# Hybrid decoder layer on one core: start-up loads split over two queues, casts ordered by hand, squares behind them

## The chip, the cores and the metric

The kernel runs on one core of a Trainium2 chip. PE is TensorE (matrix products), DVE is VectorE, ACT is ScalarE, POOL is GpSimd, SP is SyncE, which here only issues DMAs. The metric is the device time in microseconds (us) of one execution, as the median of several runs.

## The reference

One layer of a hybrid decoder for 1024 prompt tokens and 64 sample tokens (8 sequences of 8), all in float32, model width 1024. One normalised input feeds a retention mixer (8 heads, with recurrent state and gate) and a sliding-window attention (8 query heads, 2 key/value heads, window 128, ALiBi, sinks, normalised q and k). Then come an output projection, a residual, and a squared-ReLU MLP of width 4096 with its own norm and residual.

```python
hn = rms_norm(x, norm_mix_gain)
proj = hn @ w_in
q_r, k_r, v_r, g_r, q_s, k_s, v_s = jnp.split(proj, cuts, axis=-1)
o_r, new_ret = retention(q_r, k_r, v_r, ret_state, chunk)
o_r = rms_norm(o_r).reshape(b, t, RET_WIDTH) * jax.nn.silu(g_r)
q_s = rms_norm(q_s.reshape(b, t, N_SWA_HEADS, HEAD_DIM), q_norm_gain)
k_s = rms_norm(k_s.reshape(b, t, N_SWA_KV, HEAD_DIM), k_norm_gain)
...
h = x + jnp.concatenate([o_r, o_s], axis=-1) @ w_out
hf = rms_norm(h, norm_ffn_gain)
h = h + jnp.square(jax.nn.relu(hf @ w_up)) @ w_down
```

## The kernel before

**Products.** A float32 product is made of three passes in a reduced format: each operand is split into a high part (`hi`, a cast on ACT) and the rest (`lo`, a subtraction on DVE, or on POOL for some weights). `mm3` (L171 to L174) then issues hi x hi, lo x hi and hi x lo into one PSUM bank; so L172, L173 and L174 are the lines of nearly all PE work, and the name of the bank tells which product it is.

**Tiles of the front.** The 1088 tokens lie in three chunks of 384, 384 and 320 columns (`CH`), the 1024 channels in eight pieces of 128 partitions. `load_x` (L90) loads some pieces of one chunk, `wload` (L63) the weights of one block of 256 output columns: raw rows into a ring of three buffers, hi on ACT (L77), lo (L79). The first block is wq0, the first half of the attention's query weights; its 128x2048 come in four quarters q0 to q3. `split_scaled` (L134) multiplies an x piece by the norm gain `g_mix` and splits it: `hnh` on ACT (L136), `hnl` on DVE (L137). The row's rms factor is not needed for these products; it is applied later, and its input is gathered beside them: `square_sum` (L139) squares a piece on ACT (the first piece straight into `rsb`, L143; the others into `sqm`, L146) and DVE adds `sqm` to `rsb` (L147). The buffer of `sqm` is one of three (tag `ntmp`, pool `nt`), which the squares of the q products (`sqq`) share.

**Products of the front.** `proj_q` (L262) multiplies wq0 with all three chunks into banks `psq`; for each it makes on ACT a square `sqq` (L268), on DVE a scaled copy `qs` (L271), and on PE column sums `prq` (L152) of `sqq`, which DVE copies to `rq` (L286). Then the key and value weights `wkv` are loaded and split, and `proj_tok` multiplies them with the token tiles into `pst` (L307). The banks of the pool `psA` (three) are shared: the first `pst` uses the bank of the first `psq` and needs it to be emptied.

**Order of issue.** SP's queue carries all loads of the front in this order: g_mix (`cload`, L58), x piece 0, q0, x piece 1, q1, x pieces 2-3, q2, x pieces 4-5, q3, x pieces 6-7, then chunk 1 in two loads of four pieces, chunk 2 in two, and constants. ACT issues nothing there; its first instruction is the load of an activation table, with a small activation (`warm`, L86) behind it. The program's order of splits and squares is the loop at L202: the splits of a chunk, then the squares of the chunk before.

**Who sets the final order.** The kernel is built with a scheduler (`TC_KW`) that orders each engine's instructions on its own, by dependences and its estimates of durations, for the whole program. `tc.issue_after(ins)` holds an instruction behind another one. So an edit in the front can change the order in later stages whose code is the same.

**A later stage of that kind.** Between 300 and 500 us retention runs block by block, with the value products (bank `pst`, weights `wv`) between. A block loads q, k and gate (`qt`, `kt`, `gt`, L543 to L546), splits q and k (L701 to L706), makes scores `rsr`, the transposed keys `pkr` (L599), the outputs `ror`, the state update `pur` (L737), and its normalised output is transposed to `pm` (L767), gated and split (`mixrh` on ACT, `mixrl` on POOL, L779). Then the output projection begins: raw rows of W_out are loaded (`wor_raw` for the retention half, `woa_raw` for the attention half, L819), split (`wor`, `woa`, L787 and L788) and multiplied with the mixers' outputs (`mixr`, and `mixa`, which L811 loads from DRAM) into banks `pso`.

Of the kernel before, what the change touches and what calls it, by code (L numbers as in the profile page):

```python
# [11 lines left out]
F32 = mybir.dt.float32  # L12
F32R = mybir.dt.float32r
AF = mybir.ActivationFunctionType
ALU = mybir.AluOpType
# [5 lines left out]
P = 128  # L21
# [4 lines left out]
CH = ((0, 384), (384, 384), (768, 320))  # L26
# [10 lines left out]
def hymba_layer(ctx: ExitStack, tc: tile.TileContext, a: dict, o: dict):  # L37
    nc = tc.nc
# [6 lines left out]
    ring = proj.enter_context(tc.tile_pool(name="ring", bufs=2, side="right", reuse_waits="tile"))  # L45
# [5 lines left out]
    def slot3(i, dt, name, cw):  # L51
        return slot(i, dt, name)[:, : 8 * cw].rearrange("p (k n) -> p k n", k=8)
# [2 lines left out]
        t_ = hnp.tile([P, 8 * cw], F32R, tag=f"hn{x}{c}", name=f"hn{x}{c}")  # L55
        return t_.rearrange("p (k n) -> p k n", k=8)

    def cload(name):  # L58
        t_ = const.tile(list(a[name].shape), F32, name="c_" + name)
        nc.sync.dma_start(t_, a[name])  # L60
        return t_

    def wload(src, kk, name, lo_eng="p", parts=2, after=()):  # L63
        hi = ring.tile([P, 2048], F32R, tag="whi", name=name + "_hi")
        lo = ring.tile([P, 2048], F32R, tag="wlo", name=name + "_lo")
        n = 2048 // parts
        after = list(after)
        for h in range(2):
            raw = ring.tile([P, 1024], F32, tag="raw", name=f"{name}_raw{h}", bufs=3)
            for q in range(0, 1024, n):  # L70
                nc.sync.dma_start(raw[:, q : q + n], src[:, h * 1024 + q : h * 1024 + q + n])
                if after:
                    load_x(*after.pop(0))
            for q in range(0, 1024, n):
                h_, l_ = (v[:, h * 1024 + q : h * 1024 + q + n] for v in (hi, lo))
                r_ = raw[:, q : q + n]
                nc.scalar.copy(h_, r_)  # L77
                eng = nc.vector if lo_eng[(2 * h + q // n) % len(lo_eng)] == "v" else nc.gpsimd
                eng.tensor_tensor(l_, r_, h_.bitcast(F32), ALU.subtract)  # L79
        return hi.rearrange("p (k n) -> p k n", k=kk), lo.rearrange("p (k n) -> p k n", k=kk)  # L80


    ones = const.tile([P, 64], F32, name="ones")
    nc.vector.memset(ones, 1.0)
    warm = const.tile([P, 1], F32, name="warm")
    nc.scalar.activation(warm, ones[:, 0:1], AF.Silu)  # L86
    g_mix = cload("g_mix")
    xs = [slot3(6 + c, F32, f"x{c}", cw) for c, (c0, cw) in enumerate(CH)]

    def load_x(c, k, n):  # L90
        c0, cw = CH[c]
        nc.sync.dma_start(
            xs[c][:, k : k + n, :],
            a["xT"][:, 8 * c0 + k * cw : 8 * c0 + (k + n) * cw].rearrange("p (k n) -> p k n", k=n),
        )

    load_x(0, 0, 1)
    w_q0 = wload(a["w_in"][0], 8, "wq0", "v", 4, ((0, 1, 1), (0, 2, 2), (0, 4, 2)))
    load_x(0, 6, 2)
    for c in (1, 2):  # L100
        for k in (0, 4):
            load_x(c, k, 4)

    g_ffn = cload("g_ffn")
    qkg = cload("qkg")
    sinks = cload("sinks")
    ident = cload("ident")
# [25 lines left out]

    def split_scaled(src, gain, hi, lo):  # L134

        nc.scalar.activation(hi, src, AF.Copy, scale=gain)  # L136
        nc.vector.scalar_tensor_tensor(lo, src, gain, hi.bitcast(F32), ALU.mult, ALU.subtract)  # L137

    def square_sum(acc, src, k, nm):  # L139

        cw = src.shape[-1]
        if k == 0:
            nc.scalar.activation(acc, src, AF.Square)  # L143
        else:
            sq = nt.tile([P, 512], F32, tag="ntmp", name=f"sq{nm}_{k}")
            nc.scalar.activation(sq[:, :cw], src, AF.Square)  # L146
            nc.vector.tensor_tensor(acc, acc, sq[:, :cw], ALU.add)  # L147
# [23 lines left out]
    def mm3(ps, lh, ll, rh, rl, first, last, more=False):  # L171
        nc.tensor.matmul(ps, lh, rh, start=first, stop=False, skip_group_check=more)  # L172
        nc.tensor.matmul(ps, ll, rh, start=False, stop=False, skip_group_check=more)  # L173
        return nc.tensor.matmul(ps, lh, rl, start=False, stop=last, skip_group_check=more)  # L174
# [22 lines left out]
    def squares_of(c):  # L197
        c0, cw = CH[c]
        for k in range(8):
            square_sum(rsb[:, c0 : c0 + cw], xs[c][:, k, :], k, f"m{c}")  # L200

    for c, (c0, cw) in enumerate(CH):  # L202
        hi, lo = hn[c]
        for k in range(8):
            split_scaled(xs[c][:, k, :], g_mix[:, k : k + 1], hi[:, k, :], lo[:, k, :])
        if c:
            squares_of(c - 1)
    def proj_tok(t, w, ps):

        _, c, r = tok_tile(t)  # L210
        hi, lo = hn[c]
        for k in range(8):
            lh, ll = hi[:, k, r : r + 128], lo[:, k, r : r + 128]
            mm3(ps[:, :256], lh, ll, w[0][:, k, :], w[1][:, k, :], k == 0, k == 7)
        return ps
# [85 lines left out]


    w = wload(a["w_in"][2], 8, "wkv", "v")
    for t in range(9):
        off, c, r0 = tok_tile(t)
        rt = rst[:, t : t + 1]
        ps = proj_tok(t, w, psA.tile([P, 512], F32, tag="mm", name="pst"))  # L307
        sq = sp.tile([P, 128], F32, tag="hsq", name="hsq")
        nc.scalar.activation(sq, ps[:, :128], AF.Square, scale=rt)
# [24 lines left out]
        if t == 8:  # L334
            nc.vector.tensor_scalar(k8[:, 128:192], pt[:, 64:128], qkg[:, 1:2], None, ALU.mult)
            nc.vector.tensor_scalar(v8, ps[64:128, 128:256], rt[64:128], None, ALU.mult)

    proj_q(1, wload(a["w_in"][1], 8, "wq1", "v"))
    nc.sync.dma_start(o["kp"], k8[:, 0:128])
    nc.sync.dma_start(o["vp"], vs[:, 7, :])  # L340
# [102 lines left out]
    s_, r_ = rq8[:, 0:4], rq8[:, 4:8]  # L443
# [62 lines left out]
    for blk in range(4):  # L506
        w = wload(a["w_in"][3 + blk], 8, f"wqk{blk}")
# [9 lines left out]
    for blk in range(2):  # L517
        w = wload(a["w_in"][7 + blk], 8, f"wg{blk}")
# [67 lines left out]
    def value_block(t):  # L586
        vt = vts[t] = rv.tile([P, 512], F32, tag="vt", name=f"vtr{t}", bufs=5)
        _, c, r = tok_tile(t)
        ps = psA.tile([P, 512], F32, tag="mm", name="pst")
        for k in range(8):  # L590
            lh, ll = (x[:, k, r : r + 128] for x in hn[c])
            ins = mm3(ps, lh, ll, w_v[k // 4][0][:, k % 4, :], w_v[k // 4][1][:, k % 4, :], k == 0, k == 7)
        nc.scalar.activation(vt, ps, AF.Copy, scale=rst[:, t : t + 1])
        return ins.ins
# [348 lines left out]
    for t in range(5):  # L943
        if t == 0:
            for _ in range(2):
                ins = queued(ins, next, decode)
            ins = queued(ins, value_block, 3)
            for _ in range(2):
                ins = queued(ins, next, decode)
# [3 lines left out]
        if t:  # L953
            ins = queued(ins, value_block, t + 3)
# [253 lines left out]
    for g, (f0, nf) in enumerate(((0, 2), (2, 4), (6, 4), (10, 4), (14, 2))):  # L1208
# [7 lines left out]
        for i in DOWN:  # L1216
# [17 lines left out]
            for m in range(4):  # L1234
                for s in range(2):
# [143 lines left out]
```

## Time and profile before

| what | value |
|---|---|
| median of 3 runs | 1193.63 us (1193.47 to 1195.85) |
| profiled execution | 1199.06 us |
| its span in the trace | 1197.3 us |
| mean granted PE clock | 0.993 |
| instructions | 23489 |
| PE busy over the span | 98% |
| DMA over the span | 142 GB/s |

The span runs from the first to the last event of the trace; the other 1.76 us of the profiled execution lie around it. Times in the profile count from the span's start. In a row of waits or of the timeline, `<-` behind a bracket or a name tells whose end the engine waited for. SPq is SP's queue of DMA issues, PEld the loading of weights into PE.

### The profile page before, as it was taken

Reading aid. Unit: us, or ns where it says so; the run is one execution under the profiler, and the core shown is the slowest. Engines: PE = TensorE matmul, PEld = TensorE weight load, DVE = VectorE, ACT = ScalarE, POOL = GpSimd, SP = SyncE. Lnnn points to the kernel's source line nnn. Section 1 sums busy time; section 2 is a strip of 40 time slices with the busy share of each in tenths; the row PEclk is TensorE's granted clock in tenths of the full one; section 3 lists DMA queues with packets and bytes.
Section 4 is the critical chain, followed back from the end, with each engine's and each line's share of the span. In section 5 each row is a group of like instructions: output and inputs, shape, how many; then the busy total and the mean of one; then the engine's idle time right before and its main releaser. Section 6 shows DMA issues by size and latency. Waiting matters only on the chain.

```text
span 1197.3 us, 23489 instructions
## 1 busy us (share of the span) xinstructions
PE 1178.0 (98%) x9405; PEld 1129.8 (94%) x9405; DVE 842.7 (70%) x1546; ACT 513.2 (43%) x1055; POOL 491.2 (41%) x393
## 2 busy tenths in 40 slices
PE   8999999999999999998999999999999999999998
PEld 7999988988778999998999999999999999999998
DVE  7556868632356969887766766667688779897676
ACT  8343545543233437644444444444552332424231
POOL 0125333333334632456666766667372133053000
PEclk9999999999899999999999999999999999999999
DMA  7211235243226654344443444434775456553215
GB/s 245 71 62 68 92 102 174 94 134 105 76 71 222 204 166 157 120 136 137 147 150 122 147 142 147 156 127 156 245 258 164 136 170 193 172 167 104 76 58 187
DMA packets 102276, 169.44 MB, mean 142 GB/s; under 512 B 11999, under 2 KB 68255, under 8 KB 101911
## 3 DMA queue, kind: packets, MB, share of 16 engines
q1 hardware_dynamic: 88279, 123.24, 30.7%
q10 hardware_dynamic: 11328, 35.79, 9.3%
q0 software_dynamic: 2560, 8.91, 2.4%
q8 instruction: 74, 1.21, 0.4%
q14 instruction: 35, 0.29, 0.1%
HBM read 114.30 MB, written 53.61 MB: 140 GB/s over the span
## 4 chain that ended last, share of the span: by engine, by line
PE 80%; DVE 8%; DMA 4%; issue 4%; POOL 2%; ACT 2%; ACTq 0%; SPq 0%; DVEq 0%; POOLq 0%
PE psd L173 8%; PE psd L174 8%; PE psd L172 8%; PE psx L173 5%; PE psx L172 5%; PE psx L174 4%; PE pst L172 2%; PE psz L173 2%; PE psz L172 2%; PE pst L173 2%; PE psz L174 2%; PE pst L174 2%; PE psf L172 2%; PE psf L174 2%; PE pso L174 2%
## 5 line engine op out<-in xcount | busy, mean ns | idle before, releaser
L174 PE MATMUL psd<-ul,wd_w 128*128 128x272 f32 x896 | 258.6, 289 | 2.0 <-DVE ul L788 2.0
L173 PE MATMUL psd<-uh,wd_w 128*128 128x272 f32 x896 | 259.9, 290 | 0.4 <-DVE wd_w L788 0.4
L172 PE MATMUL psd<-uh,wd_w 128*128 128x272 f32 x896 | 258.6, 289 | 0.6 <-ACT uh L787 0.6
L174 PEld LDWEIGHTS psd<-ul,wd_w 128*128 128x128 f32 x896 | 169.2, 189 | 2.9 <-DVE ul L788 2.9
L172 PEld LDWEIGHTS psd<-uh,wd_w 128*128 128x128 f32 x896 | 169.8, 189 | 0.8 <-ACT uh L787 0.8
L173 PEld LDWEIGHTS psd<-uh,wd_w 128*128 128x128 f32 x896 | 169.1, 189 | 0.8 <-DVE wd_w L788 0.7
L1248 DVE TENSOR_TENSOR a<-a,psd 128x272 f32<-128x272 f32 x248 | 101.4, 430 | 41.9 <-PE psd L174 41.8
L788 DVE TENSOR_TENSOR wu_w<-wu_s,wu_w 128x512 fp32r<-128x512 f32 x64 | 61.8, 967 | 52.5 <-ACT wu_w L787 51.7
L787 ACT CAST wd_w<-wd_s 128x512 fp32r<-128x512 f32 x64 | 37.3, 618 | 111.4 <-PE psd L174 99.3
L788 DVE TENSOR_TENSOR ul<-ur,uh 128x1088 fp32r<-128x1088 f32 x56 | 83.5, 1520 | 1.7 <-ACT uh L787 1.7
L172 PE MATMUL psx<-op_1h,wu_w 128*128 128x272 f32 x256 | 74.3, 290 | 3.0 <-ACT m L1125 3.0
L1111 DVE SCALAR_TENSOR_TENSOR m<-m,rsf 128x272 f32<-128x272 f32 x96 | 74.1, 771 | 3.1 <-ACT rsf L910 0.5
L173 PE MATMUL psx<-op_1h,wu_w 128*128 128x272 f32 x256 | 74.7, 292 | 0.0
L173 PE MATMUL psx<-op_0h,wu_w 128*128 128x272 f32 x256 | 74.5, 291 | 0.0
L174 PE MATMUL psx<-op_1l,wu_w 128*128 128x272 f32 x256 | 74.3, 290 | 0.0
L172 PE MATMUL psx<-op_0h,wu_w 128*128 128x272 f32 x256 | 74.0, 290 | 0.3 <-ACT m L1125 0.3
L174 PE MATMUL psx<-op_0l,wu_w 128*128 128x272 f32 x256 | 74.0, 289 | 0.0
L787 ACT CAST uh<-ur 128x1088 fp32r<-128x1088 f32 x56 | 59.7, 1101 | 15.4 <-PE psd L173 9.1
L362 POOL TENSOR_TENSOR sp<-sp,ssp 128x1024 f32<-128x1024 f32 (+1 forms) x16 | 28.6, 1787 | 88.4 <-DVE ssp L361 60.0
L172 PE MATMUL psf<-hnh,wqk_hi 128*128 128x384 f32 (+1 forms) x192 | 63.5, 331 | 0.2 <-DVE qkst L514 0.2
L174 PE MATMUL psf<-hnl,wqk_hi 128*128 128x384 f32 (+1 forms) x192 | 63.1, 329 | 0.0
L173 PE MATMUL psf<-hnh,wqk_lo 128*128 128x384 f32 (+1 forms) x192 | 62.8, 327 | 0.0
(342 smaller groups left out, 3629.2 us busy)
## 6 DMA issues: line engine op xcount, KB each, us to landing
ur<-u_d SPq DMA_DIRECT2D x52, 544.0 KB, 5.0
u_d<-r4t SPq DMA_DIRECT2D x32, 544.0 KB, 4.3
wu_r<-in_w_up ACTq DMA_DIRECT2D x32, 512.0 KB, 4.4
wd_r<-in_w_down ACTq DMA_DIRECT2D x30, 512.0 KB, 6.6
u_d<-r3t SPq DMA_DIRECT2D x32, 408.0 KB, 2.7
y<-in_xY POOLq DMA_DIRECT2D x16, 272.0 KB, 3.5
y_d<-y POOLq DMA_DIRECT2D x16, 272.0 KB, 2.9
yt<-y_d SPq DMA_DIRECT2D x16, 272.0 KB, 3.5
```

What stands on the lines that cost most here:

```text
L172: nc.tensor.matmul(ps, lh, rh, start=first, stop=False, skip_group_check=more)
L173: nc.tensor.matmul(ps, ll, rh, start=False, stop=False, skip_group_check=more)
L174: return nc.tensor.matmul(ps, lh, rl, start=False, stop=last, skip_group_check=more)
L362: nc.gpsimd.tensor_tensor(s, s, ss.unsqueeze(2).broadcast_to([P, 4, n]), ALU.mult)
L787: nc.scalar.copy(hi, src)
L788: lo_eng.tensor_tensor(lo, src, hi.bitcast(F32), ALU.subtract)
L1111: nc.vector.scalar_tensor_tensor(t_, src, 0.0, rsf[:, s, h, :], ALU.max, ALU.mult)
L1248: nc.vector.tensor_tensor(to, to, ps, ALU.add)
```

## The change

It does five things in the code of the front:

1. `g_mix` and the quarters q0 and q1 are loaded from ACT's queue, ahead of its table load; the other loads stay on SP, in the order x piece 0, x piece 1, q2, x pieces 2-3, q3, x pieces 4-5, x pieces 6-7.
2. Chunk 1 is loaded in three parts: pieces 0-1, 2-3, 4-7.
3. The hi casts of the first chunk and of wq0 are chained on ACT by `issue_after` in the order x0, q0, x1, q1, x2, x3, q2, x4, x5, q3, x6, x7.
4. The squares of a chunk may be issued only behind the last of these casts.
5. `wload` loses the argument that put x loads between its own.

```diff
-    def cload(name):
+    def cload(name, eng=nc.sync):
         t_ = const.tile(list(a[name].shape), F32, name="c_" + name)
-        nc.sync.dma_start(t_, a[name])
+        eng.dma_start(t_, a[name])
...
+    g_mix = cload("g_mix", nc.scalar)
+    raw_q0 = [ring.tile([P, 1024], F32, tag="raw", name=f"wq0_raw{h}", bufs=3) for h in range(2)]
+
+    def load_q0(q, eng):
+        eng.dma_start(raw_q0[q // 2][:, q % 2 * 512 : q % 2 * 512 + 512], a["w_in"][0][:, q * 512 : q * 512 + 512])
+
+    for q in (0, 1):
+        load_q0(q, nc.scalar)
     ones = const.tile([P, 64], F32, name="ones")
     nc.vector.memset(ones, 1.0)
     warm = const.tile([P, 1], F32, name="warm")
     nc.scalar.activation(warm, ones[:, 0:1], AF.Silu)
-    g_mix = cload("g_mix")
...
     load_x(0, 0, 1)
-    w_q0 = wload(a["w_in"][0], 8, "wq0", "v", 4, ((0, 1, 1), (0, 2, 2), (0, 4, 2)))
+    load_x(0, 1, 1)
+    load_q0(2, nc.sync)
+    load_x(0, 2, 2)
+    load_q0(3, nc.sync)
+    load_x(0, 4, 2)
     load_x(0, 6, 2)
-    for c in (1, 2):
-        for k in (0, 4):
-            load_x(c, k, 4)
+    for c, k, n in ((1, 0, 2), (1, 2, 2), (1, 4, 4), (2, 0, 4), (2, 4, 4)):
+        load_x(c, k, n)
...
-    for c, (c0, cw) in enumerate(CH):
+    def split_x(c, k):
         hi, lo = hn[c]
+        return split_scaled(xs[c][:, k, :], g_mix[:, k : k + 1], hi[:, k, :], lo[:, k, :])
...
+    def split_q0(q):
+        h_, l_ = (v[:, q * 512 : q * 512 + 512] for v in (wq_hi, wq_lo))
+        r_ = raw_q0[q // 2][:, q % 2 * 512 : q % 2 * 512 + 512]
+        ins = nc.scalar.copy(h_, r_)
+        nc.vector.tensor_tensor(l_, r_, h_.bitcast(F32), ALU.subtract)
+        return ins.ins
+
+    ins = split_x(0, 0)
+    for f_, args in (
+        (split_q0, (0,)), (split_x, (0, 1)), (split_q0, (1,)), (split_x, (0, 2)), (split_x, (0, 3)), (split_q0, (2,)),
+        (split_x, (0, 4)), (split_x, (0, 5)), (split_q0, (3,)), (split_x, (0, 6)), (split_x, (0, 7)),
+    ):
+        with tc.issue_after(ins):
+            ins = f_(*args)
+    w_q0 = [v.rearrange("p (k n) -> p k n", k=8) for v in (wq_hi, wq_lo)]
+    for c in (1, 2):
         for k in range(8):
-            split_scaled(xs[c][:, k, :], g_mix[:, k : k + 1], hi[:, k, :], lo[:, k, :])
-        if c:
+            split_x(c, k)
+        with tc.issue_after(ins):
             squares_of(c - 1)
```

What the scheduler makes of it shows in the order of the instructions. In the following rows a number behind a name is a buffer's, and lines of the changed kernel lie some 30 below those of the kernel before.

DVE at the end of the front, before: the adds of chunk 1's squares (`sqm_3` to `sqm_7`), the last x splits, the two halves of `wkv_lo`, and the first copies `qs`.

```order
L147 TENSOR_TENSOR rsb<-rsb,sqm_3_249 128x384
L137 SCALAR_TENSOR_TENSOR hnl_165<-x_77,c_g_mix,hnh_164 128x320 x4
L147 TENSOR_TENSOR rsb<-rsb,sqm_4_252 128x384
L137 SCALAR_TENSOR_TENSOR hnl_165<-x_77,c_g_mix,hnh_164 128x320 x4
L147 TENSOR_TENSOR rsb<-rsb,sqm_5_255 128x384
L79 TENSOR_TENSOR wkv_lo<-wkv_raw_612,wkv_hi 128x1024
L147 TENSOR_TENSOR rsb<-rsb,sqm_6_258 128x384
L79 TENSOR_TENSOR wkv_lo<-wkv_raw_616,wkv_hi 128x1024
L235 MEMSET q2v 128x512
L147 TENSOR_TENSOR rsb<-rsb,sqm_7_261 128x384
L271 TENSOR_SCALAR qs_267<-psq,qg_115 128x384 x2
```

The same place after:

```order
L155 TENSOR_TENSOR rsb<-rsb,sqm_1_244 128x384
L144 SCALAR_TENSOR_TENSOR hnl_156<-x_81,c_g_mix,hnh_155 128x320 x4
L155 TENSOR_TENSOR rsb<-rsb,sqm_2_247 128x384
L76 TENSOR_TENSOR wkv_lo<-wkv_raw_613,wkv_hi 128x1024
L76 TENSOR_TENSOR wkv_lo<-wkv_raw_617,wkv_hi 128x1024
L155 TENSOR_TENSOR rsb<-rsb,sqm_3_250 128x384
L155 TENSOR_TENSOR rsb<-rsb,sqm_4_253 128x384
L155 TENSOR_TENSOR rsb<-rsb,sqm_5_256 128x384
L264 MEMSET q2v 128x512
L155 TENSOR_TENSOR rsb<-rsb,sqm_6_259 128x384
L300 TENSOR_SCALAR qs_268<-psq,qg_106 128x384
L155 TENSOR_TENSOR rsb<-rsb,sqm_7_262 128x384
```

The adds no longer stand one by one between splits but three in a row behind `wkv_lo`, and the last one stands behind the first `qs`. Further up, the adds 1, 2, 3 and 4, 5 of chunk 0 also stand in a row now, behind all splits of that chunk; before, only 2 and 3 did, and the add of `sqm_1` stood between the splits of pieces 1 and 2. On ACT the squares 3 to 7 of chunk 1 stand in a row between the second cast of `wkv_hi` and the first `sqq`; before, they alternated with x splits and the two casts.

SP where W_out's first rows are loaded, before:

```order
L544 DMA kt_4088<-kr_d 128x4x128
L546 DMA gt_4091<-g_d 128x4x128
L543 DMA qt_4243<-qr_d 128x4x128
L819 DMA wor_0_raw<-in_w_out 128x2x512
L819 DMA woa_0_raw<-in_w_out 128x2x512
L811 DMA mixah_4226<-ms_hi_d 128x4x544
L811 DMA mixal_4228<-ms_lo_d 128x4x544
L544 DMA kt_4244<-kr_d 128x4x128
L819 DMA woa_2_raw<-in_w_out 128x2x512
L546 DMA gt_4247<-g_d 128x4x128
```

and after:

```order
L572 DMA qt_4244<-qr_d 128x4x128
L573 DMA kt_4245<-kr_d 128x4x128
L575 DMA gt_4248<-g_d 128x4x128
L848 DMA wor_0_raw<-in_w_out 128x2x512
L848 DMA woa_0_raw<-in_w_out 128x2x512
L840 DMA mixah_4227<-ms_hi_d 128x4x544
L840 DMA mixal_4229<-ms_lo_d 128x4x544
L572 DMA qt_4462<-qr_d 128x4x128
```

The key and gate loads of the next block (`kt_4245`, `gt_4248`) went ahead of W_out's first rows and of the attention output. A key load waits until PE has transposed the block whose buffer it takes, a gate load until POOL has done `mixrl` of an earlier block.

PE at the first product with W_out, before:

```order
L174 MATMUL pst<-wv_lo,hnh_164 128x512
L767 MATMUL pm<-c_ident,mtr_3924 128x128 x4
L599 MATMUL pkr_3997<-c_ident,kt_3968 128x128 x4
L722 MATMUL ror_4004<-vtr_3606,rptr_3986 64x64 x8
L722 MATMUL ror_4004<-vtr_3606,rptr_3995 64x64 x8
L730 MATMUL ror_4004<-state_3386,qdr_4021 128x128 x4
L737 MATMUL pur_4027<-vtr_3606,kdr_4002 64x64 x8
L172 MATMUL pso<-mixrh,wor_0_4218 128x272
```

and after, from the transposes `pkr` on:

```order
L628 MATMUL pkr_3998<-c_ident,kt_3969 128x128 x4
L751 MATMUL ror_4005<-vtr_3607,rptr_3987 64x64 x8
L751 MATMUL ror_4005<-vtr_3607,rptr_3996 64x64 x8
L759 MATMUL ror_4005<-state_3387,qdr_4022 128x128 x4
L182 MATMUL pst<-wv_lo,hnh_155 128x512
L180 MATMUL pst<-wv_hi,hnh_155 128x512
L181 MATMUL pst<-wv_hi,hnl_156 128x512
L182 MATMUL pst<-wv_lo,hnh_155 128x512
L766 MATMUL pur_4028<-vtr_3607,kdr_4003 64x64 x8
L180 MATMUL rsr_4256<-qkb 128x256
L180 MATMUL rsr_4265<-qkb 128x256
```

Four value products and the scores `rsr` of the next block (ten more of its products follow) now lie between the transposes and the first `pso`.

More of the change, by code (lines that the diff above doesn't have):

```diff
@@ L56, in hn_tile, with wload @@
         return t_.rearrange("p (k n) -> p k n", k=8)
-    def cload(name):
+    def cload(name, eng=nc.sync):
         t_ = const.tile(list(a[name].shape), F32, name="c_" + name)
-        nc.sync.dma_start(t_, a[name])
+        eng.dma_start(t_, a[name])
         return t_
-    def wload(src, kk, name, lo_eng="p", parts=2, after=()):
+    def wload(src, kk, name, lo_eng="p", parts=2):
         hi = ring.tile([P, 2048], F32R, tag="whi", name=name + "_hi")
@@ L66, in wload @@
         n = 2048 // parts
-        after = list(after)
         for h in range(2):
@@ L71, in wload @@
                 nc.sync.dma_start(raw[:, q : q + n], src[:, h * 1024 + q : h * 1024 + q + n])
-                if after:
-                    load_x(*after.pop(0))
             for q in range(0, 1024, n):
@@ L134, in split_scaled @@
     def split_scaled(src, gain, hi, lo):
-        nc.scalar.activation(hi, src, AF.Copy, scale=gain)
+        ins = nc.scalar.activation(hi, src, AF.Copy, scale=gain)
         nc.vector.scalar_tensor_tensor(lo, src, gain, hi.bitcast(F32), ALU.mult, ALU.subtract)
+        return ins.ins
     def square_sum(acc, src, k, nm):
@@ L200, in squares_of @@
             square_sum(rsb[:, c0 : c0 + cw], xs[c][:, k, :], k, f"m{c}")
-    for c, (c0, cw) in enumerate(CH):
+    def split_x(c, k):
         hi, lo = hn[c]
+        return split_scaled(xs[c][:, k, :], g_mix[:, k : k + 1], hi[:, k, :], lo[:, k, :])
+    wq_hi, wq_lo = (ring.tile([P, 2048], F32R, tag="w" + x, name="wq0_" + x) for x in ("hi", "lo"))
+    def split_q0(q):
[3 more added lines that the diff above has]
+        nc.vector.tensor_tensor(l_, r_, h_.bitcast(F32), ALU.subtract)
+        return ins.ins
+    ins = split_x(0, 0)
[7 more added lines that the diff above has]
+    for c in (1, 2):
         for k in range(8):
-            split_scaled(xs[c][:, k, :], g_mix[:, k : k + 1], hi[:, k, :], lo[:, k, :])
-        if c:
+            split_x(c, k)
+        with tc.issue_after(ins):
             squares_of(c - 1)
```

## The prediction

> **What bounds the kernel now.** I read the page's engine line first, then the busy time by stretches of the span, because a share over 1197 us says nothing about the first 40, where the change works.
>
> ```profile
> PE 1178.0 (98%) x9405; PEld 1129.8 (94%) x9405; DVE 842.7 (70%) x1546; ACT 513.2 (43%) x1055; POOL 491.2 (41%) x393
> ```
>
> The columns of the stretches are: length, then busy time (and instructions) of PE, PEld, DVE, ACT and POOL, then the granted clock, the DMA share and GB/s.
>
> ```profile
> 0.00:5.00 5.00, 3.67 (x36) 3.53 (x36) 0.56 (x3) 2.52 (x4) 0.82 (x15) 1.00 0.48 123
> 5.00:10.00 5.00, 2.87 (x13) 2.06 (x14) 2.79 (x6) 3.06 (x6) 0.00 (x0) 1.00 0.94 313
> 10.00:20.00 10.00, 9.75 (x50) 8.27 (x50) 9.90 (x20) 10.00 (x22) 0.00 (x0) 1.00 1.02 387
> 20.00:25.00 5.00, 4.57 (x25) 3.58 (x25) 5.00 (x13) 5.00 (x13) 0.00 (x0) 1.00 0.72 244
> 30.00:35.00 5.00, 3.84 (x78) 3.43 (x77) 3.10 (x8) 0.49 (x1) 0.00 (x0) 1.00 0.63 207
> 40.00:80.00 40.00, 40.00 (x413) 39.24 (x411) 27.99 (x94) 21.23 (x51) 13.15 (x14) 1.00 0.18 56
> 360.00:400.00 40.00, 38.43 (x380) 34.35 (x379) 28.30 (x60) 14.15 (x25) 19.25 (x16) 0.96 0.78 256
> ```
>
> From 40 us on PE is never idle for long (40.00 of 40.00), so nothing later swallows a delay of PE, and nothing later returns one. The front decides by how much PE enters that stretch late. There, between 10 and 25 us, DVE (9.90, 5.00) and ACT (10.00, 5.00) are full, PE is not (20 to 25 us: 4.57). The chain that ended last and PE's waits say which of them sets the end of the front:
>
> ```profile
> 3.09 6.10 DMA x<-in_xT
> 9.21 0.62 ACT hnh L136
> 9.86 1.15 DVE hnl L137 x2
> 11.00 0.48 DVE rsb L147
> ...
> 31.03 0.41 DVE rsb L147
> 31.44 0.53 DVE qs L271
> 32.02 0.39 PE pst L172
> ```
>
> ```profile
> PE pst L172 <- DVE qs L271: 1.2, 1, 1.2
> ```
>
> PE stands 1.2 us until DVE has emptied the first q accumulator (qs), whose PSUM bank the first key/value product (pst) needs. DVE comes to that copy late because it works through a list without a gap from 9.86 us, and that start hangs on the load of x pieces 2 and 3, issued at 3.09 and landed 6.10 later, at 9.19. So the front is a DVE list of fixed length behind one load. It is not a matter of when PE sees its first operands.
>
> **The front, part by part.** What the list holds, and what preceded it:
>
> ```profile
> 7.57 0.55 DVE L147 TENSOR_TENSOR rsb<-rsb,sqm 128x384 f32<-128x384 f32 x1
> ...
> 10.92 1.21 DVE L147 TENSOR_TENSOR rsb<-rsb,sqm 128x384 f32<-128x384 f32 x2
> ...
> 28.80 0.55 DVE L147 TENSOR_TENSOR rsb<-rsb,sqm 128x384 f32<-128x384 f32 x1
> 29.27 1.22 DVE L79 TENSOR_TENSOR wkv_lo<-wkv_raw,wkv_hi 128x1024 fp32r<-128x1024 f32 x1
> ```
>
> *Length of the list.* The change removes no DVE or ACT instruction before the first pst; it reorders them. Before, one add of squares was done at 7.57, in time in which the loads had DVE waiting anyway, and all seven adds of chunk 1 stood ahead of qs: 13 adds inside the list. Now no add precedes x pieces 2 and 3, and the seventh of chunk 1 stands behind qs: 7 + 6 = 13 again. The items are the same, so this part costs 0. What was gained by pushing one add behind qs pays for the filler that the early gap lost.
>
> *Adds in a row.* An add needs the sum of the one before. Two in a row take 1.21 us (10.92), while one followed by other work leaves the next instruction to start 0.47 after it (28.80 to 29.27) and is itself 0.55 long: 1.02 for a pair. A pair in a row thus costs 0.19 more. Before, one pair stood so (2, 3); now five do (1-2, 2-3, 4-5, and 3-4, 4-5 of chunk 1). Four more: 4 x 0.19 = +0.76. Ends: 0 if other work hides it, 0.76.
>
> *The squares start later on ACT.*
>
> ```profile
> L137 DVE SCALAR_TENSOR_TENSOR hnl<-x,c_g_mix,hnh 128x384 fp32r<-128x384 f32 (+1 forms) x24 | 13.2, 591 | 4.6 <-ACT hnh L136 4.6
> ...
> L146 ACT ACTIVATE sqm<-x 128x384 f32<-128x384 f32 x14 | 6.8, 511 | 0.0
> ```
>
> After the last hi cast of chunk 0 ACT makes two squares, about 2 x 0.51, before DVE can do its first add; DVE has only one hnl (0.59) to do meanwhile. If DVE carries no backlog there, it stands 0.4; with some backlog nothing. I take +0.2.
>
> *The load that starts the list.* In bytes, an x piece of 128x384 is 0.197 MB, a weight quarter of 128x512 0.262 MB. Before, up to and with pieces 2-3: 2 x 0.197 + 2 x 0.262 + 0.393 = 1.31 MB; now q2 goes ahead of them as well: 1.57 MB. At the 313 GB/s of 5 to 10 us the extra 0.262 MB cost 0.84. Against it, pieces 2-3 are SP's fourth issue instead of its sixth, two issues of 0.47 each earlier:
>
> ```profile
> 1.20 0.42 SPq L92 DMA_DIRECT2D x<-in_xT  x1
> 1.67 0.42 SPq L71 DMA_DIRECT2D wq_raw<-in_w_in  x1
> ...
> 3.09 0.43 SPq L92 DMA_DIRECT2D x<-in_xT  x1
> ```
>
> That gives -0.1; at the mean of 0 to 10 us, (123 + 313)/2 = 218 GB/s, 1.20 - 0.94 = +0.26. I take +0.2. The other ends: +1.2, if issuing earlier gains nothing; and, if two queues brought the rate to the 387 GB/s of 10 to 20 us from 5 us on, 0.615 MB (123 x 5) are there by then and the other 0.955 take 2.5 us: landed at 7.5, -1.7. No row of before shows two queues at once in this place. The Trainium skill speaks against the gain ("DMA: Bandwidth & Descriptors", section "Issuing engines are not separate DMA queues"): DMAs started by several engines run on the same 16 DMA engines and interleave, and only the issuing time is saved. By that rule the term stays near +0.2, without it it is -1.7; no run so far shows which.
>
> *The scale and the first two quarters on ACT* cost ACT three issues ahead of its table load. Its first hi cast was at 3.91 us, waiting for a DMA, so three issues of 0.47 before it lie beside that wait: 0. With that wait gone they would cost up to 1.4.
>
> *The accumulators' squares (sqq).* ACT now has five squares in a row behind the second key/value cast, and the three buffers that they share with sqq are freed by the adds; the third sqq waits for the add that now stands behind qs. PE needs it for its third set of column sums, soon after the first pst. I put +0.2 on PE (0 to 0.5).
>
> Front: 0 + 0.76 + 0.2 + 0.2 + 0 + 0.2 = **+1.4** (main bounds +0.3 to +2.3). The third load of chunk 1 adds one SP issue of 0.47 to a queue that runs ahead of use: 0.
>
> **W_out, 340 us later.** The scheduler also orders another stage anew. Before, the first rows of W_out were issued some 13 us ahead of their use:
>
> ```profile
> 365.03 0.61 SPq L819 DMA_DIRECT2D wor_raw<-in_w_out  x1
> ```
>
> ```profile
> 367.26 0.51 PE L172 MATMUL rsr<-qk,qk 128*128 128x256 f32 x2
> ...
> 368.92 0.28 PE L174 MATMUL rsr<-qk,qk 128*128 128x256 f32 x1
> ...
> 371.55 0.39 PE L173 MATMUL pst<-wv_hi,hnl 128*128 128x512 f32 x1
> 371.78 0.39 PE L174 MATMUL pst<-wv_lo,hnh 128*128 128x512 f32 x1
> ...
> 374.05 0.60 PE L767 MATMUL pm<-c_ident,mtr 128*128 128x128 f32 x4
> ...
> 377.80 0.39 PE L172 MATMUL pso<-mixrh,wor 128*128 128x272 f32 x1
> ...
> 380.75 0.36 PE L172 MATMUL pso<-mixah,woa 128*128 128x272 f32 x1 [1.13 <-DMA mixah<-ms_hi_d]
> ...
> 382.28 0.39 PE L173 MATMUL pso<-mixrh,wor 128*128 128x272 f32 x1 [0.44 <-DVE wor L788]
> ```
>
> Now wor stands on SP behind a gate load (gt), whose buffer comes free when POOL has done mixrl. That ended at 376.12 + 1.26 = 377.38, and would now be 4 x 0.23 = 0.92 earlier, because four value products that stood ahead of pm stand behind it: 376.46. Then gt's issue (some 0.6), so wor issues at about 377.1.
>
> ```profile
> 376.12 1.26 POOL L779 TENSOR_TENSOR mixrl<-gt,mixrh 128x512 fp32r<-128x512 f32 x1 [0.50 <-ACT mixrh L778]
> ```
>
> ```profile
> L787 ACT CAST wor<-wor_raw x16: 614/621/629, 375.9 to 489.6; 128x512 fp32r<-128x512 f32 x16
> ...
> DMA to landing us min/median/max: 3.5/4.9/8.1
> ```
>
> With 3.5 to 4.9 to land and 0.62 to cast, wor is ready at 381.2 to 382.6. PE gets to the first pso at 377.80 plus a block's scores (rsr), which it now does first (367.26 to 369.20, less the 0.39 of a pst among them: 1.55): 379.35. So it waits 1.9 to 3.3. The waits of 1.13 and 0.44 that it had lie in the shadow of that, or stay: the net is +0.3 to +2.2, and I take +1.2. The mixer's loads, behind wor now, are reached after that wait, twelve pso products and another block's transposes and outputs, and I count no wait for them.
>
> **Sum.** +1.4 + 1.2 = +2.6 on PE, and so on the end. The profiled execution took 1199.06 us, with a span of 1197.3 and 1.76 around it, at 1201.7 after; it lies 5.4 over the median of the runs, so I put the difference on the median: 1193.63 + 2.6 = **1196.2**. A measurement of this kernel can tell 0.2% (2.4 us) from no change, so the forecast is just beyond the border, at 1196.0.
>
> **Rivals.**
> *Two queues feed the front faster (not slower).* For it: between 5 and 10 us the DMA engines are busy 0.94 of the time and move 313 GB/s, at 1.02 387, so some packets are slow there. Against it: one queue reaches 387 alone a little later. Price: -1.7 in place of +0.2 makes the front -0.5, the time 1194.3 (with an even W_out 1193.1; if W_out's old waits of 1.57 went too, 1191.6). It decides if pieces 2-3 are cast before about 8.9 us, 0.3 ahead of now.
> *W_out hides its own delay.* If wor lands in the time that the pulled-up scores give, the new wait only replaces the old ones: +1.4, 1195.0. For it: SP's queue and the DMA engines are nearly empty there; against: landing in 3.5 still leaves 1.9.
> *W_out late by a full queue.* At the longest landing, 8.1, wor is ready at 385.8, a wait of 6.5 less 1.57: +4.9, in all +6.3, 1199.9.
> *The loads on ACT do not start early.* If they only started after a table load of some 1.3 us, q1, which ACT casts ahead of pieces 2-3, would hold those by about 0.7: 1196.9.
>
> **How the numbers follow.** Forecast 0.46, and since the border lies inside its own bounds, 0.28 of it slower and 0.18 the same. W_out hidden 0.18: 0.14 same, 0.04 faster. Fast queues 0.21: 0.08 same, 0.13 faster (only with W_out also gaining). Late W_out 0.10 and late loads 0.05: slower. Faster 0.17, same 0.40, slower 0.43. The range leaves out the far part of late W_out above 1199.2 (0.1) and the far part of fast queues below 1191.0 (0.1). The forecast's own bounds are 1193.63 + 0.3 + 0.3 = 1194.2 to 1193.63 + 2.3 + 2.2 = 1198.1.
>
> **What would show it.** Right: the cast of pieces 2-3 near 9.2 to 9.6; DVE full from there to qs, which starts near 32.5; first pst near 33.2, still waiting for qs; PE's first q products earlier than before, without effect; a wait of 2 to 3 us at the first pso, for wor. Wrong: a first pst at or before 32.0 (the load or the list was mis-sized), adds in a row at 0.47 spacing, PE going from pur to pso without a wait, or a difference that arises between 40 and 300 us or behind 460, where I count on none.

## The result, and the profile after

The changed kernel takes 1204.85 us in the median of 6 runs (1202.41 to 1207.07), the kernel before 1194.10 beside it (1191.39 to 1195.85): a ratio of 1.0085, 95% interval 1.0070 to 1.0099. The medians differ by 10.75 us (10.1 by the ratio), where 2.6 were forecast and 1199.2 was the upper end. The profiled execution took 1204.71 us, its span is 1202.9.

**The front.** The chain that ended last, at the same place as in the prediction:

```profile
1.67 7.45 DMA wq_raw<-in_w_in
9.14 0.62 ACT wq_hi L219
9.76 1.02 ACT hnh L143 x2
...
28.34 0.43 ACT sqm L154
28.79 1.22 DVE wkv_lo L76
30.01 0.48 DVE rsb L155
...
32.77 0.53 DVE qs L300
33.34 0.39 PE pst L180
```

The list now starts behind q1, which came from ACT's queue at 9.12, not behind x pieces 2-3, and the first pst starts at 33.34, 1.32 later than before. Up to 28.77 it now runs on ACT, but DVE is as full as before (no gap over 0.10 from 9.79 on). DVE's rows show the adds in a row, ACT's rows what they hold up:

```profile
29.93 1.88 DVE L155 TENSOR_TENSOR rsb<-rsb,sqm 128x384 f32<-128x384 f32 x3
...
32.68 0.60 DVE L300 TENSOR_SCALAR qs<-psq,qg 128x384 f32<-128x384 f32 x1
```

```profile
30.51 1.18 ACT L154 ACTIVATE sqm<-x 128x384 f32<-128x384 f32 x2 [0.92 <-DVE rsb L155]
31.90 0.49 ACT L297 ACTIVATE sqq<-psq 128x384 f32<-128x384 f32 x1 [0.20 <-DVE rsb L155]
32.88 0.88 ACT L297 ACTIVATE sqq<-psq 128x384 f32<-128x384 f32 x2 [0.49 <-DVE rsb L155]
```

Three adds take 1.88, so each that follows another costs (1.88 - 0.55)/2 = 0.67 instead of 0.47. Through the three shared buffers ACT waits for them (0.92), and the first sqq starts at 31.90; before the change the first two started at 29.04. So PE now waits twice, first for ACT:

```profile
PE prq L160 <- ACT sqq L297: 2.5, 1, 2.5
...
PE pst L180 <- DVE qs L300: 0.4, 1, 0.4
```

What follows was in no part of my sum. In these rows of after, the 384-wide products of the second q block are 0.32 apart and 0.52 long until 38.1, then 0.17 apart and 0.33 long:

```profile
36.24 0.52 PE L180 MATMUL psq<-hnh,wq_hi 128*128 128x384 f32 x1
36.56 0.52 PE L181 MATMUL psq<-hnh,wq_lo 128*128 128x384 f32 x1
...
38.12 0.33 PE L180 MATMUL psq<-hnh,wq_hi 128*128 128x384 f32 x1
38.29 0.34 PE L181 MATMUL psq<-hnh,wq_lo 128*128 128x384 f32 x1
```

The granted clock (third number from the end) says why; first after, then before:

```profile
32.00:34.00 2.00, 1.03 (x29) 0.97 (x30) 2.00 (x6) 1.26 (x3) 0.00 (x0) 1.00 0.64 236
34.00:36.00 2.00, 2.00 (x54) 1.61 (x53) 1.12 (x4) 0.00 (x0) 0.00 (x0) 0.66 0.05 12
36.00:38.00 2.00, 2.00 (x9) 2.00 (x8) 0.00 (x0) 0.00 (x0) 0.00 (x0) 0.50 0.00 0
38.00:40.00 2.00, 2.00 (x13) 2.00 (x12) 0.00 (x0) 0.00 (x0) 0.00 (x0) 0.99 0.00 0
```

```profile
34.00:36.00 2.00, 2.00 (x37) 1.85 (x36) 0.17 (x1) 0.00 (x0) 0.00 (x0) 1.00 0.04 14
36.00:38.00 2.00, 2.00 (x14) 2.00 (x13) 0.00 (x0) 0.00 (x0) 0.00 (x0) 1.00 0.00 0
```

PE counts as busy in both, but after the change it runs at half clock from 34.6 to 38.1: 3.4 us in which 1.7 are lost. The first psf shows both losses together: 84.9 against 81.7, +3.2.

**W_out.** The waits that the reorder was to bring are there, and again half a clock behind them:

```profile
383.38 0.39 PE L181 MATMUL rsr<-qkb 128*128 128x256 f32 x1 [0.85 <-POOL qkb L731]
...
385.83 0.39 PE L180 MATMUL pso<-mixrh,wor 128*128 128x272 f32 x1 [1.00 <-ACT wor L816]
386.56 0.59 PE L181 MATMUL pso<-mixrh,wor 128*128 128x272 f32 x1 [0.34 <-DVE wor L817]
...
391.60 0.66 PE L796 MATMUL pm<-c_ident,mtr 128*128 128x128 f32 x2 [2.17 <-DVE mtr L644]
```

```profile
380.00:390.00 10.00, 6.98 (x47) 5.46 (x45) 4.34 (x13) 3.41 (x7) 5.83 (x6) 0.81 0.86 291
390.00:400.00 10.00, 8.40 (x83) 7.77 (x84) 6.29 (x16) 2.90 (x6) 3.82 (x3) 0.68 1.07 372
```

Before, the same 20 us read:

```profile
380.00:390.00 10.00, 8.81 (x85) 7.98 (x87) 4.79 (x9) 1.74 (x3) 4.20 (x4) 0.83 1.07 360
390.00:400.00 10.00, 10.00 (x114) 9.70 (x109) 9.85 (x21) 4.28 (x8) 5.31 (x5) 1.00 0.99 328
```

In these two executions before is at half clock for 3.4 us here (382.9 to 386.3), after for 10.2 us on end (386.2 to 396.5). From the first psf to the MLP's first product (psx) it is 425.3 us after and 419.8 before; the first start stands behind the three durations, after, then before:

```profile
L180 PE MATMUL psf<-hnh,wqk_hi x192: 302/334/441, 84.9 to 223.8; 128*128 128x384 f32 x128, 128*128 128x320 f32 x64
...
L180 PE MATMUL psx<-op_0h,wu_w x256: 283/289/393, 510.2 to 852.2; 128*128 128x272 f32 x128
```

```profile
L172 PE MATMUL psx<-op_0h,wu_w x256: 283/288/428, 501.5 to 845.3; 128*128 128x272 f32 x128
```

### The profile page after: what moved, and what is told of

Same layout as the page of the kernel before. It is cut to its first block, busy times and chain, and to the rows that moved or that the text cites. A ratio compares the mean times of both kernels' runs of the same rounds, so it can differ in the third digit from the quotient of the medians.

```text
span 1202.9 us, 23488 instructions
## 1 busy us (share of the span) xinstructions
PE 1179.1 (98%) x9405; PEld 1131.7 (94%) x9405; DVE 837.0 (70%) x1546; ACT 513.0 (43%) x1055; POOL 489.7 (41%) x393
## 4 chain that ended last, share of the span: by engine, by line
PE 80%; DVE 7%; issue 4%; DMA 3%; ACT 3%; POOL 3%; ACTq 0%; SPq 0%; DVEq 0%; POOLq 0%
PE psd L181 8%; PE psd L182 8%; PE psd L180 8%; PE psx L180 5%; PE psx L182 5%; PE psx L181 5%; PE pst L180 2%; PE psz L180 2%; PE psz L182 2%; PE psz L181 2%; PE pst L181 2%; PE pst L182 2%; PE psf L180 2%; PE psf L182 2%; PE psf L181 2%
## 5 line engine op out<-in xcount | busy, mean ns | idle before, releaser
L817 DVE TENSOR_TENSOR ul<-ur,uh 128x1088 fp32r<-128x1088 f32 x56 | 84.2, 1533 | 0.5 <-ACT uh L816 0.5
```

What stands on the lines that cost most here:

```text
L817: lo_eng.tensor_tensor(lo, src, hi.bitcast(F32), ALU.subtract)
```

## The experiments

The ratios are against the kernel before, run beside each; its median was 1192.9 to 1194.3. Theory A: the squares behind the casts cost 1.3 us at the first pst and some 1.9 by the clock, W_out's new order the rest. Rival B: the two queues cost the front, and W_out's waits follow from it.

**squares_behind**: all loads back on SP in the old order, cast order and squares as changed; W_out's loads stood as before.

```diff
-    for q in (0, 1):
-        load_q0(q, nc.scalar)
...
-    load_x(0, 0, 1)
-    load_x(0, 1, 1)
-    load_q0(2, nc.sync)
+    load_x(0, 0, 1)
+    load_q0(0, nc.sync)
+    load_x(0, 1, 1)
+    load_q0(1, nc.sync)
```

> The changed kernel with all loads of the front on SP in the old order; the cast order and the squares behind it stay, and W_out's loads stand on SP as before the change. Theory A (the squares behind the casts cost 1.3 us at the first pst and some 1.9 by a halved PE clock after the long wait; W_out's new order costs some 5.5 on its own): first pst near 33.3, psf starts 1.3 to 3.3 us later than before, first pso waits no longer than before, +1.3 to +3.4 us in all. Rival B (the front's loss comes from the two queues, q1 landing at 9.1 instead of 8.0, and W_out's waits follow from a late front): first pst at 32.0 and 0 us.

1200.08 us, ratio 1.0058 (1.0041 to 1.0074). First pst at 32.77, half clock right behind it, psf at 85.3, +3.6:

```profile
31.96 0.50 PE L160 MATMUL prq<-halves,sqq 128*32 128x2 f32 x24 [2.50 <-ACT sqq L297]
32.77 0.58 PE L180 MATMUL pst<-wkv_hi,hnh 128*128 128x256 f32 x1 [0.31 <-DVE qs L300]
```

The front's loss is there without the second queue; rival B falls for the front. In the median it is more than theory A's range (some +7 against +3.4 at most), in the trace a little above its upper end (+3.8 at the first psx).

**two_queues**: the loads and the chained casts as changed, the squares free.

```diff
-        with tc.issue_after(ins):
-            squares_of(c - 1)
+        squares_of(c - 1)
```

> The changed kernel with its loads on two queues and its chained casts, but the squares free to stand between them; W_out's loads stand on SP as before the change. Theory A: q1 lands late as in the changed kernel, but ACT fills that time with squares; first pst 31.5 to 32.5, -0.5 to +0.5 us in all, no halved clock at 35 us. Rival B: first pst at 33 or later, +3 us.

1194.80 us, ratio 1.0006 (0.9992 to 1.0021): no difference. First pst at 31.22 and no half clock, although q1 also lands late here (cast at 8.15 behind a wait of 1.52, and pieces 2-3 cast at 8.94):

```profile
30.58 0.37 PE L160 MATMUL prq<-halves,sqq 128*32 128x2 f32 x24 [0.68 <-ACT sqq L296]
31.22 0.39 PE L180 MATMUL pst<-wkv_hi,hnh 128*128 128x256 f32 x1 [0.27 <-DVE qs L299]
```

The squares, free again, fill the time in which the loads hold ACT. The first pst stood 0.8 earlier than before in this profile. In two_queues_spare (below), whose front is the same, q1 was cast at 8.98 and pieces 2-3 at 9.76, as late as in the changed kernel; there the first pst stood at 32.0, as before the change, again without a half clock. So late loads alone cost the front nothing there, and no gain by the two queues can be told either.

**wout_pinned**: the changed kernel, with the old order of loads at W_out.

```diff
+        with tc.issue_after(behind) if behind else ExitStack():
+            nc.sync.dma_start(kt, kr_d[:, :, off : off + 128])
+            last_load[0] = nc.sync.dma_start(gt, g_d[:, :, off : off + 128])
...
-        qt, kt, gt = ret_load(t)
+        qt, kt, gt = ret_load(t, mixed.ins if t == 5 else None)
```

> The changed kernel, front untouched, but the key and gate loads of block 5 are held behind the first loads of W_out and of the attention output, as they stood before the change. Theory A: the front is as in the changed kernel (psf +3.3), the first pso waits no more than before, and 5 to 6 us of the 10 come back: +3 to +4.5 us against before. Rival B (the waits at W_out follow from the late front, or were there already): +9 to +10 us.

1200.68 us, ratio 1.0065 (1.0046 to 1.0084), where the changed kernel has 1.0085 (1.0070 to 1.0099): the medians alone leave open how much comes back. The trace is plainer: from psf to psx it is 418.8 us, less than before the change (419.8), where the changed kernel takes 425.3. PE still waits 2.2 at the first pso, but no half clock follows:

```profile
380.00:390.00 10.00, 7.80 (x92) 6.79 (x91) 7.36 (x18) 3.97 (x7) 6.11 (x6) 1.00 0.74 238
390.00:400.00 10.00, 10.00 (x93) 9.79 (x92) 7.31 (x18) 3.63 (x8) 6.15 (x6) 1.00 1.08 360
```

**wout_swapped**: the kernel before, with block 5's loads ahead of W_out's.

```diff
+    pre5 = ret_load(5)
     gens = {x: wo_pair(0, 0, x) for x in "ra"}
-    ahead = [next(gens[x]) for x in "ra"][::-1]
-    mix_load(0, mx0)
+    with tc.issue_after(last_load[0].ins):
+        ahead = [next(gens[x]) for x in "ra"][::-1]
+        mix_load(0, mx0)
```

> The kernel before, front untouched, but block 5's q, key and gate are loaded ahead of W_out's first rows and of the attention output, as in the changed kernel. Theory A: first pst at 32.0 as before; first pso waits for wor by 1 to 3 us, PE's clock is halved for some us afterwards; +4.5 to +6.5 us. Rival B: 0 to +1 us, since the front is on time.

1197.04 us, ratio 1.0040 (1.0021 to 1.0059), 4.1 in the medians. The order at W_out costs time with a front that is on time; rival B falls here too. The wait stood elsewhere than expected: PE waited for the scores' operands (2.3 for ACT, 0.8 for POOL), since those also load later. In the profiled execution, the fastest of its nine (1193.96), the first psx stood at 501.4, as in the first profile of before, so this trace doesn't show the loss that the median has. The half clock at W_out did come, and for 6.8 us (378.1 to 384.9); but the one that the first profile of before has at 321.5 to 328.3 is absent here, and so is the one in the MLP.

**spare_products**: the changed kernel, PE given 12 products that nothing reads where it waits for sqq.

```diff
+                if blk == 0 and c == 2 and jj == 1:
+                    with tc.issue_after(last_q[0].ins):
+                        for _ in range(12):
+                            ins = nc.tensor.matmul(wps[:, :384], w[0][:, 0, :128], hn[0][0][:, 0, :], start=True, stop=True)
```

> The changed kernel with 12 spare products (128x384, into an unused bank, read by nothing) on PE behind the last product of wq0, where it stood idle for 2.5 us; W_out's order is the changed kernel's. Theory A (the long empty stretch of PE halves its clock from 34.4 to 38.2 us): the granted clock stays at 1.00 from 30 to 40 us, first pst as late as before (33.3), psf starts at 83.0 instead of 84.9, 1.5 to 2.5 us faster than the changed kernel, +8 to +9.5 us against before. Rival C (the clock falls for another reason, the loads or the work before): clock 0.6 to 0.7 at 35 us again and no change.

```profile
30.00:35.00 5.00, 4.14 (x92) 3.47 (x91) 4.37 (x11) 2.37 (x5) 0.00 (x0) 1.00 0.53 178
35.00:40.00 5.00, 5.00 (x33) 5.00 (x33) 0.02 (x1) 0.54 (x2) 0.00 (x0) 1.00 0.00 0
```

1200.92 us, ratio 1.0051 (1.0034 to 1.0068), 0.34% or 4 us less than the changed kernel's. The clock stays at 1.00, psf starts at 82.9. The first pst was at 32.79, 0.55 earlier than in the changed kernel; of the 2.0 us at psf the clock thus accounts for some 1.5. Rival C falls for the front, by this one profile: with PE's wait filled the clock doesn't halve, and work that computes nothing makes the kernel faster.

**squares_late**: the kernel before, the squares of chunk 1 behind the first q projection.

```diff
-        if c:
-            squares_of(c - 1)
+        if c == 1:
+            squares_of(0)
...
     proj_q(0, w_q0)
+    squares_of(1)
     squares_of(2)
```

> The kernel before with one edit: the squares of chunk 1 follow the whole first q projection in the program, so that no add of them stands ahead of qs. Theory A (a list of fixed length on DVE and ACT sets the first pst): seven adds of 0.47 and seven squares of 0.41 less ahead of it, first pst at 30.0 to 30.7, right behind the last product of wq0, psf 1.2 to 2 us earlier, -1 to -3 us. Rival D (the squares are only moved to where the key products wait for the row norms): PE waits in pst or behind, 0 to +2 us.

1197.48 us, ratio 1.0016 (0.9999 to 1.0033): not faster, probably slower. The front gained: PE had no wait left from 20 to 60 us, and psf started at 80.2, 1.5 earlier. (The first pst stood at 34.3, since other products went ahead of it.) It had been lost again by the end of the gate products behind the attention (last psg begins at 285.9, before at 285.3). The scheduler had changed that stage's order as well, and PE waited 1.2 us more from 200 to 240; squares_late, then before:

```profile
200.00:240.00 40.00, 38.84 (x245) 34.52 (x244) 27.91 (x65) 21.79 (x53) 12.81 (x6) 1.00 0.34 111
```

```profile
200.00:240.00 40.00, 40.00 (x253) 35.78 (x252) 28.08 (x70) 23.55 (x61) 12.27 (x6) 1.00 0.35 115
```

**changed_squares_late** and **changed_late_pinned**: the same edit in the changed kernel, the second with wout_pinned's edit besides.

> The changed kernel with the squares of chunk 1 behind the whole first q projection in the program; W_out's order stays the changed kernel's. Theory A: the front is mended (first pst at 31 or earlier, no halved clock at 35), W_out's loss stays: +3 to +6 us against before. Rival B (W_out's loss follows from the late front): 0 or less.

> The same as the changed kernel with late squares, and block 5's key and gate loads held behind W_out's first loads and the attention output's, as before the change. Theory A: both losses are gone, -2 to +1 us against before. Rival (the two queues or the chain cost on their own): +2 us or more.

1206.37 us, ratio 1.0088 (1.0067 to 1.0109), and 1201.01, 1.0052 (1.0036 to 1.0068). Both expectations fell. The first pst came at 30.7 and 30.3 with the clock at 1.00, as expected, but psf at 84.7 and 84.2: PE lost 2.4 us between, in waits for DVE and ACT, which have the late squares and their adds to do there (42.6 to 58.4). That these made the waits is likely, but not shown.

```profile
40.00:60.00 20.00, 19.00 (x226) 18.12 (x225) 14.91 (x45) 9.07 (x20) 5.03 (x6) 1.00 0.17 54
60.00:80.00 20.00, 18.61 (x161) 17.89 (x161) 13.55 (x50) 11.32 (x30) 7.85 (x8) 1.00 0.15 41
```

Pinning W_out gave back 5.4 us in this pair, timed on the same chip.

**changed_wout_spare**, **before_spare**, **two_queues_spare**: spare products meant for waits further on. They go into unused columns of a bank whose sum is still open and start a sum of their own there; part of that open sum is lost, so the layer's output y lacks some products with W_out (and, in the last two, of the MLP).

```diff
+                if m == 0 and h == 0 and n == 0:
+                    with tc.issue_after(last_out[0].ins):
+                        for _ in range(18):
+                            ins = nc.tensor.matmul(
+                                full[0][:, Q:512], w[:, 0, 0:128], mix[0, "rh"][:, 0, 0, :240], start=True, stop=True, skip_group_check=True)
+                    spare.append(ins.ins)
```

> The changed kernel with 18 spare products (128x240, into unused columns of a bank, read by nothing) on PE behind the first products with W_out, where it then waited 2.2 us for pm. Theory A (part of W_out's loss is the halved clock that follows PE's waits): the half clock from 391 to 395 us is gone, psx starts 1.5 to 2.5 us earlier than in the changed kernel (507.7 to 508.7), -1.5 to -2.5 us against it, +8 to +9 us against before. Rival C (the clock there falls whatever PE does): half clock again after 391, 0.

1204.77 us, ratio 1.0085 (1.0071 to 1.0098), no faster. From psf to psx it took 423.6 us, 1.7 less than in the first profile of the changed kernel; the wait for pm was gone, and the half clock shorter (0.88 and 0.95 in the two windows above, 3.4 us in all) but not gone. Since the changed kernel's second profile (below) has 421.7 without spare products, this run decides nothing.

> The kernel before with spare products in two waits of PE that it has: 10 (128x240) behind the first products with W_out, where it waits 1.1 us for mixah, and 22 ahead of the fourth pair of up-products, where it waits 3.0 us for ACT (539.7 to 542.9). Theory A: no half clock behind either (382 to 386, 543 to 547), which costs some 1.7 us each in the executions in which it falls there; the waits themselves stay or grow by 0.1; mean granted clock up by 0.001 to 0.003, -1 to -3 us. Rival C: the same clock, 0 to +0.5 us.

> The same two sets of spare products in the kernel with the loads on two queues, chained casts and free squares. Theory A: first pst at 31.2 as without them, no half clock behind the two waits, -1 to -3.5 us against before. Rival C: 0 to +1 us.

1193.41 us, ratio 1.0000 (0.9987 to 1.0013), and 1193.57, 0.9998 (0.9989 to 1.0007): no gain. Before, PE's wait of 3 us in the MLP has the half clock behind it; before_spare shows none there:

```profile
540.00:542.00 2.00, 0.00 (x0) 0.00 (x0) 1.92 (x2) 0.00 (x1) 1.62 (x2) 1.00 0.00 0
542.00:544.00 2.00, 1.11 (x6) 1.11 (x7) 0.61 (x1) 1.97 (x5) 0.00 (x0) 0.83 0.82 276
544.00:546.00 2.00, 2.00 (x11) 2.00 (x10) 1.56 (x4) 0.79 (x4) 0.00 (x0) 0.50 0.78 264
```

```profile
515.91 2.65 PE L1144 MATMUL psx<-op_0h,wu_w 128*128 128x240 f32 x22
...
538.00:540.00 2.00, 0.30 (x3) 0.08 (x1) 1.97 (x6) 0.70 (x2) 0.00 (x0) 1.00 0.51 207
540.00:542.00 2.00, 2.00 (x16) 2.00 (x17) 0.63 (x2) 1.59 (x4) 0.00 (x0) 1.00 1.06 359
```

But the 22 products don't stand in the wait: they ran at 515.9, over 20 us ahead of it, and the wait itself was 1.7 us long here and 1.4 in two_queues_spare. So these two runs don't show what filling the wait in the MLP does. The 10 products at W_out did take the place of PE's wait for mixah. In two_queues_spare the clock stayed at 1.00 up to 1190 us, and yet the time is that of before; the 32 spare products took PE some 3.6 us themselves. No version here beats the kernel before.

**before_again**, **squares_behind_again**, **wout_pinned_again**, **changed_again**: a second profile of four kernels, to place what the first pairs left open.

> The kernel before, unchanged, for a second profile. Theory A: first pst at 32.0, psf at 81.7, first psx within 1 us of 501.5; behind it the time to the end differs from the first profile's 691.4 by the number of half-clock stretches alone, and is 686 to 691.

> The changed kernel with all loads on SP in the old order, for a second profile. Theory A (the loss lies ahead of the MLP): psf 3 to 4 us behind before's, psx 4 to 6 behind, the rest as long as before's. Rival E (a late front also makes the MLP longer): psx no more than 4 behind, the MLP 2 to 3 us longer.

> The changed kernel with block 5's key and gate loads held behind W_out's, for a second profile. Theory A: psf 3 to 4 us and psx 3 to 5 us behind before's; rest as long. Rival E: MLP 2 to 3 us longer.

> The changed kernel for a second profile. Theory A: psf 3 to 4 us behind before's, psx 8 to 10 us behind, the rest as long as before's. Rival E: psx at most 8.7 behind, MLP 2 us longer.

| start of (us) | before | squares_behind | wout_pinned | changed |
|---|---|---|---|---|
| first psf | 81.7, 81.6 | 85.3, 86.1 | 85.8, 85.5 | 84.9, 85.1 |
| first psx | 501.5, 499.0 | 505.3, 504.6 | 504.6, 504.1 | 510.2, 506.8 |
| first psx to last psd | 691.4, 689.6 | 690.3, 689.8 | 693.2, 692.4 | 688.3, 688.1 |

At W_out the changed kernel's second profile has one half-clock stretch, before's second has none:

```profile
380.00:390.00 10.00, 7.28 (x49) 5.70 (x47) 5.48 (x15) 3.97 (x7) 6.07 (x6) 0.83 0.85 288
390.00:400.00 10.00, 9.57 (x111) 9.12 (x111) 8.04 (x20) 3.08 (x5) 4.19 (x3) 1.00 1.07 370
```

```profile
380.00:390.00 10.00, 8.82 (x103) 8.06 (x102) 5.36 (x12) 1.74 (x3) 6.26 (x5) 1.00 1.10 348
390.00:400.00 10.00, 10.00 (x117) 9.55 (x116) 9.83 (x18) 5.20 (x10) 4.57 (x5) 1.00 0.81 275
```

The front's half clock was there in all six profiles of these kernels with the squares behind the casts, and in neither of before. In five of the six it lasted 6.8 us, twice as long as in the first profile of the changed kernel. Its second profile:

```profile
30.00:32.00 2.00, 0.37 (x24) 0.40 (x24) 1.83 (x5) 1.17 (x4) 0.00 (x0) 0.90 0.90 283
32.00:38.00 6.00, 5.69 (x75) 5.13 (x68) 2.32 (x7) 0.85 (x2) 0.00 (x0) 0.50 0.11 42
```

There the first pst came at 32.4 and psf still at 85.1. Rival E (a longer MLP) falls for the changed kernel and squares_behind; wout_pinned's MLP is 2 us longer: in its first profile PE waits 2.3 us more there than in before's, and why stays open. In the mean of two profiles the changed kernel is 8.3 us behind at psx, against 10.75 in the medians, squares_behind 4.7 against 7.2; the remaining 2.5 us I can't place with two profiles each.

## Why the prediction was wrong

- **The chain and its list: right.** First pst forecast near 33.2, measured 33.34 and, in the second profile, 32.4. The list's items are the same 13 adds, and a pair in a row costs 0.20 where 0.19 was taken.
- **The load: near in size, other cause.** The cast of pieces 2-3 began at 9.67 instead of 9.21 (+0.46, forecast +0.2), but at 8.72 in the second profile, so its size is one execution's. In the first, not pieces 2-3 were late but q1, from the second queue, behind which they are now chained; I had that as a rival at +0.7, for another reason. q1, now the second of its queue, landed at 9.12, where it had been fourth in one queue and there at 7.96; over all profiles it was cast at 8.15 to 9.14 in the ten with two queues and at 7.57 to 8.13 in the seven with one. That agrees with what the Trainium skill states ("DMA: Bandwidth & Descriptors", section "Issuing engines are not separate DMA queues"): a second issuing engine feeds the same DMA engines and saves issuing time only.
- **The squares on ACT: far too small.** I put +0.2 on sqq, for the third. The first was late already: the five squares and their buffers, freed by adds in a row, held it to 31.90, and PE stood 2.5 for it. The first pst was not later for that, since qs held it; what the wait cost came through the clock.
- **The step that failed: "on PE, and so on the end".** I priced a wait of PE at its length. I read that PE is never idle for long from 40 us on, from a row that ends at 80 us (it waits 1.1 at 380 and 3.0 at 540), and that nothing returns a delay, but not that its speed depends on what was ahead. The wait put PE at half clock for 3.4 us in the first profile and 6.8 in the second: from the first pst to psf it took 1.9 and 3.0 us more than before, where nothing was forecast, and 1.4 for the whole front. Before's own trace shows the pattern: a granted clock of 0.83 from 380 to 390 us, behind waits of 1.1 and 0.4, and half clock behind the wait of 3.0 at 540 (rows above). My quoted window of 360 to 400 had 0.96 in it, and I passed over it. The Trainium skill has the mechanism ("TensorE: Matmul & The Clock Gate", section "Part 1: The HAM clock gate (the "warmup" mystery)"): the clock drops to half after an idle window of some 3.4 us and rises after a busy one. The traces agree on the half and on the length (3.41 us or a multiple of it); they differ on the gap, since a wait of 2.5 us, with small products behind it, was enough, and in one execution of two the 1.1 and 0.4 at 380 us. The same page of the Trainium skill, section "HAM oscillation — how this bites in real kernels", would have let a gap of 2.5 pass.
- **W_out: mechanism right, size wrong.** The waits for wor came, 1.0 + 0.34, less than the 1.9 to 3.3 forecast; others that I hadn't listed came too: 0.26 + 0.85 for the pulled-up scores, 2.17 for pm. In sum 4.6 against 1.6 before, +3.0 where +1.2 was taken, and then the clock: +5.5 in this profile, +4.3 in the second against before's second. The pinned order takes it away, with the front as late as in the changed kernel.
- **The rivals.** "Two queues feed faster" fell: alone they bring the first pst 0.8 earlier in one profile and no earlier in the other, with nothing left of it at the end. Late W_out (1199.9) was the nearest in size, by another way.

## What to carry to other kernels

Price a wait of PE at its length plus, once it reaches 2 to 3 us (or several smaller ones stand close, or small products around it), half of the time at half clock that can follow, here up to 1.7 or 3.4 us; look at the granted clock behind every wait of the old trace before adding up. Filler work that an engine does while loads hold it is not in the way: moving it behind the critical casts left the list as long as it was and took the filler from the gap. And where a scheduler orders the whole program, an edit in the front is two changes; compare the order everywhere, and pin what shouldn't move before judging the edit.

## What the runs showed of the hardware

Behind the wait of 2.5 us in the front, PE ran at half clock in seven of seven profiles; behind its wait of 3.0 us in the MLP, which the kernels without spare products there all have, in 12 of 15.

It also matters when the wait falls. Within each trace all changes of the granted clock lie on one grid of 3.41 us, which starts elsewhere in every execution, and a half clock lasts one step of it or several: in the front 3.4 us in one of the seven profiles and 6.8 in six. The grid tells the 15 profiles of the MLP apart: in the 12 with the half clock at least 1.94 us of the wait lie within one step, in the other three at most 1.83. That isn't a rule for every place. In the first profile of the changed kernel the front's wait was split into 1.2 and 1.3 us, and the half clock came all the same, behind 24 products of two columns each (prq). And no wait is needed: in before's second profile the clock is halved from 308.5 to 311.9, though PE counts as busy from 300 to 314, behind 16 products of 64 columns and 16 of 32.

Part of the spread between executions comes from this: the two profiled ones of before were at half clock for 17.1 and 6.8 us and took 1199.06 and 1194.76.

With spare products over 2.1 of the 2.5 us in the front the half clock didn't come (one profile). For the MLP no run shows it.

A product that starts a sum in other columns of a bank seems to end the sum still open there: the output y of three kernels lacked part of it. The Trainium skill states it ("PSUM — Partial Sum Buffer", section "The four PSUM rules"): a first product clears the marks for accumulation over the whole bank in the partitions that it writes. The outputs agree; no run isolates it.
